# Low parts of 32 expert chunks made beside the merges and read back from DRAM

## The chip, the cores and the metric

The kernel runs on one core of a Trainium2 chip. The core has TensorE (PE, matrix products), VectorE (DVE), ScalarE (ACT) and GpSimd (POOL), each with an instruction queue of its own that is worked off in order; SyncE (SP) only issues transfers. The metric is device microseconds of one execution, less being better; a kernel's time is the median of its runs.

## The reference, cut to what matters

Two transformer blocks in float32. The first mixes a latent attention and a retention branch and then has a layer of 16384 experts, of which each token uses 128 (8 heads x 16). For 512 tokens:

```python
merged = jax.nn.sigmoid(za) * y_a + jax.nn.sigmoid(zr) * y_r
h = h + merged @ w_mix_out
x = rmsnorm(h, g_ffn)
q = (x @ w_peer_q).reshape(T, 8, 128)
# eidx, gates: the 16 best of 128 x 128 pairs of keys for each head
act = gelu(einsum('td,tkd->tk', xt, peer_u[it]))
y = einsum('tk,tkd->td', gt * act, peer_v[it])
```

## The kernel before

Every product is made in float32r, as three products of a high and a low part: an operand's high part is the operand cast to float32r (`hi`), its low part the rest (`lo = x - hi`), and the product is hi x hi + hi x lo + lo x hi. For a weight, `weights` (L226) loads 512 KB into a raw tile, ScalarE casts it to `hi` (L212), and DVE or GpSimd subtracts for `lo` (L213). Raw, high and low tiles have two buffers each. `flip` sends the low parts of ordinary weights to DVE and GpSimd in turn.

The first block runs in this order. After the attention and retention branches (to about 360 us) come the merges: for each of eight chunks of 128 output columns, four weights (`w_za`, `w_mla`, `w_zr`, `w_ret`) are loaded, split and multiplied, and the two gated sums are added and split into `mg` (L873). Then come the mix product with `h1` (the residual, loaded into two slots of the pool `sp_`, which has ten), the norm, and the expert layer's queries.

In the expert layer, the three groups of 128 tokens 0 to 2 are computed densely: all 128 chunks of 128 experts are multiplied (`front`: 24 products of 128 x 384 for one chunk of u, then GELU), weighted with a gate matrix and multiplied with the chunk of v. For the fourth group, 128 rows of u and 128 rows of v are gathered for every token by GpSimd's indirect transfers, and used on DVE (`g_u`, `g_v`).

From about 600 to 1000 us the experts are picked: `topkeys` and `topk` find the best keys (on DVE), and `spread` makes the gate matrices: DVE makes one-hot rows (`oh`, L1111), ScalarE or DVE scales them (L1114, L1116), PE multiplies them (L1119), ScalarE copies the result, and it is stored to DRAM. Beside this run the fronts of chunks 0 to 67, spaced by a count of steps; their low parts of u are all made on GpSimd (`u_of(e, G)`). `fm` reads the low part last, in the third eight of the 24 products.

From about 1040 us the expert loop runs: fronts of the other chunks, products with v, gathers. The order of its instructions on DVE, ScalarE and GpSimd is written out by hand; elsewhere the order of each engine's instructions is settled when the kernel is built. Where one engine needs another's result, it waits on a semaphore, and so does everything behind it in its queue.

Of the kernel before, what the change touches and what calls it, by code (L numbers as in the profile page):

```python
# [9 lines left out]
F32 = mybir.dt.float32  # L10
F32R = mybir.dt.float32r
# [3 lines left out]
OP = mybir.AluOpType  # L15
AX = mybir.AxisListType

P = 128
# [4 lines left out]
D = 1024  # L23
KD = D // P
# [142 lines left out]
def build(tc, A, OUT):  # L167
    nc = tc.nc
    es = ExitStack()
    V, S, G, TE = nc.vector, nc.scalar, nc.gpsimd, nc.tensor  # L170

    def pool(name, bufs=1, stack=es, **kw):
        if kw.get("space") != bass.MemoryType.DRAM:
            kw["reuse_waits"] = "tile"
        return stack.enter_context(tc.tile_pool(name=name, bufs=bufs, **kw))

    cp = pool("cst")
    dp = pool("dram", space=bass.MemoryType.DRAM)
# [10 lines left out]
    def mmps(name="mm"):  # L189
        return bank("mm", name)  # L190
# [14 lines left out]
    ones_sq = cp.tile([P, P], F32, name="ones_sq")  # L205
    G.memset(ones_sq, 1.0)

    flip = [0]

    def split(src, hi, lo, lo_eng=None):  # L210

        S.copy(hi, src)  # L212
        (lo_eng or V).tensor_tensor(lo, src, hi.bitcast(F32), op=OP.subtract)  # L213
# [6 lines left out]
    def load(ap, n, tag="w", queue=nc.sync):  # L220
        wp, words, bufs = wts[tag]
        raw = wp.tile([P, words], F32, name=tag + "r", bufs=bufs)
        queue.dma_start(raw[:, :n], ap)
        return raw

    def weights(ap, n, lo_pool=3, tag="w", raw=None):  # L226

        wp, words, bufs = wts[tag]
        raw = raw or load(ap, n, tag)
        hi = wp.tile([P, words], F32R, name=tag + "h", bufs=2)  # L230
        lo = wp.tile([P, words], F32R, name=tag + "l", bufs=2)
        flip[0] += 1
        if isinstance(lo_pool, int):
            lo_pool = V if flip[0] % lo_pool else G
        split(raw[:, :n], hi[:, :n], lo[:, :n], lo_pool)
        return hi, lo

    def kview(pair, kt, width):
        return tuple([t[:, k * width:(k + 1) * width] for k in range(kt)] for t in pair)

    def wfm(name, c, kt=KD, width=P, c0=0):

        n = kt * width
        return kview(weights(A[name][c][:, c0:c0 + n], n, 2), kt, width)

    def mm3(out, l, r, first, last):
        (lh, ll), (rh, rl) = l, r
# [4 lines left out]
    def fm(out, w, act, c0, t0, n, kt=KD, hooks=(), late=0):  # L252


        for tiles in (range(kt - late), range(kt - late, kt)):
            for i, (a, b) in enumerate(((0, 0), (1, 0), (0, 1)) if late else ((0, 0), (0, 1), (1, 0))):
                for k in tiles:
                    TE.matmul(out, w[a][k][:, c0:c0 + P], act[b][k][:, t0:t0 + n],  # L258
                              start=i == 0 and k == 0, stop=i == 2 and k == kt - 1)
                if i < len(hooks) and not late:  # L260
                    hooks[i]()
            if not late:
                break
# [31 lines left out]
    def ks(t):  # L295

        return [t[:, k] for k in range(t.shape[1])]
# [147 lines left out]
    def two(tp, name="t2", dt=F32):  # L445

        return tp.tile([P, L], dt, name=name, tag="t2")
# [4 lines left out]
    def halves(name, tag, dt=F32):  # L452
        h = [xp.tile([P, 4, L], dt, name=name, tag=tag, bufs=2) for _ in range(2)]
        return h, [h[k // 4][:, k % 4] for k in range(KD)]
# [18 lines left out]
    def half_slot(name, dt=F32):  # L473
        return sp_.tile([P, 4, L], dt, name=name, tag="h")

    def flat(t, n):
        return t.rearrange("p k t -> p (k t)")[:, :n]

    def mtwo(name="m2"):
        return tp.tile([P, L], F32, name=name, tag="m2", bufs=9)  # L480

    src = A["hT"].rearrange("p (k t) -> p k t", k=KD)
    _, h1 = halves("h1", "xa")
# [4 lines left out]
    with tc.manual_schedule(engines={mybir.EngineType.DVE, mybir.EngineType.Activation}):  # L488
        raws = [load(A["w_cq"][0], D, queue=nc.scalar)]
        for k in range(KD):  # L490
            (nc.scalar if k % 2 else nc.sync).dma_start(h1[k], src[:, k])
        raws.append(load(A["w_cq"][1], D))
        wqs = []
        for k in range(KD):
            g = gcol[:, G_MIX + k:G_MIX + k + 1]
            S.activation(u[0][k], h1[k], AF.Copy, scale=g)
            V.scalar_tensor_tensor(u[1][k], h1[k], g, u[0][k].bitcast(F32), op0=OP.mult, op1=OP.subtract)
            if k in (1, KD - 1):
                wqs.append(kview(weights(None, D, V, raw=raws[k // 2 and 1]), KD, P))
# [40 lines left out]
    c = ks(half_slot("ckv", F32R))  # L540
# [6 lines left out]
    x = mtwo()  # L547
# [8 lines left out]
    for t0, t1, m in ((0, NT, P), (NT, NT + 1, M)):  # L556
        h = t1 - t0
        pv = pt[:m, t0 * 32:t1 * 32].rearrange("p (t d) -> p t d", t=h)
        x = mtwo()
# [84 lines left out]
    for h in range(8):  # L644
        b = 64 - h % 2 * 64
# [4 lines left out]
    def fm_pieces(w, pieces):  # L650

        x = two(t2)
        for a, b in pieces:
            ps = mmps()
            fm(ps[:, :b - a], w, hn, 0, a, b - a)
            S.copy(x[:, a:b], ps[:, :b - a])
        return x
# [110 lines left out]
    for h in range(8):  # L768
        x = fm_pieces(wfm("w_rv", h), PIECES)
# [10 lines left out]
        b = h % 2 * 64  # L780
# [65 lines left out]
    for h in range(8):  # L846
        w = wfm("w_rg", h)
# [10 lines left out]
    def gate(name, c, x):  # L858

        w = wfm(name, c)  # L860
        ps = mmps()
        fm(ps, w, hn, 0, 0, T)
        S.activation(x, ps, AF.Tanh, scale=0.5)
        return x

    def gated(name, c, act, kt, x):

        w = wfm(name, c, kt)
        ps = mmps()
        fm(ps, w, act, 0, 0, T, kt)  # L870
        V.scalar_tensor_tensor(x, x, 1.0, ps, op0=OP.add, op1=OP.mult)

    def merged(a, b, mg, d):  # L873
        G.tensor_tensor(a, a, b, op=OP.add)
        S.activation(mg[0][d], a, AF.Copy, scale=0.5)
        V.scalar_tensor_tensor(mg[1][d], a, 0.5, mg[0][d].bitcast(F32), op0=OP.mult, op1=OP.subtract)

    mg = tuple([x for _ in range(2) for x in ks(half_slot(n, F32R)[:, :, :T])] for n in ("mgh", "mgl"))
    for c in range(KD):
        x = gate("w_za", c, two(t2)[:, :T])  # L880
        gated("w_mla", c, oT, 4, x)
        y = gate("w_zr", c, two(t2)[:, :T])
        gated("w_ret", c, yr, KD, y)
        merged(x, y, mg, c)
    sty.close()
    h1 = [x for _ in range(2) for x in ks(half_slot("h1"))]
    for k in range(KD):
# [68 lines left out]
    acts, done_u = {}, []  # L956

    def u_of(e, eng=V):
        return kview(weights(A["u_T"][e], D, eng), KD, P)

    def act_tile(e, side):
        return (tr if side else tp).tile([P, TD], F32, name="act", bufs=15 if side else 19)
# [373 lines left out]
    kt = pool("keytmp", stack=stk)  # L1336
# [22 lines left out]
    for x in range(2):  # L1359
# [8 lines left out]
        for hf in range(2):  # L1368
            w = sp_.tile([P, 8, 256], F32, name="wc1", tag="h")
            nc.sync.dma_start(w.rearrange("p l c -> p (l c)"), A["w_c1"][x][:, hf * 2048:(hf + 1) * 2048])  # L1370
            w1.append(w)
    for br in range(2):
        w = wfm("w_kv", 2 * br)
# [4 lines left out]
        for g in range(2):  # L1378
            a, b = slice(g * 64, g * 64 + 64), slice(64 - g * 64, 128 - g * 64)
# [4 lines left out]
        w = wfm("w_kv", 2 * br + 1)  # L1384
        ps = mmps()
        fm(ps, w, hn, 0, 0, T)
        x = two(t2)[:, :T]
# [8 lines left out]
    w = wfm("w_gn", 0, width=48)  # L1396
# [3 lines left out]
    x = two(t2)[:48, :T]  # L1400
# [158 lines left out]
    for g in range(4):  # L1559
        w = wfm("w_u", g)  # L1560
# [32 lines left out]
    for c in range(KD):  # L1593
        y = gate("w_gm", KD + c, two(t2)[:, :T])
        gated("w_pn", c, ysl, KD, y)
        x = gate("w_gm", c, two(t2)[:, :T])
# [19 lines left out]
    w = kview(weights(A["w_f1"][0], KD * 256, tag="ww"), KD, 256)  # L1616
# [11 lines left out]
    for b in range(4):  # L1628
        f = tuple(ks(slot(n, F32R)) for n in ("fh", "fl"))
        for c in range(4):  # L1630
            if b or c:
                w = kview(weights(A["w_f1"][4 * b + c], KD * 256, tag="ww"), KD, 256)
# [52 lines left out]
```

## Time and profile before

| | |
|---|---|
| median of three runs | 2686.99 us (2679.85 to 2689.2) |
| profiled execution | 2676.28 us |
| its span, first to last instruction | 2674.5 us |
| busy: PE, DVE, ACT, POOL | 2579.5, 1713.8, 1145.0, 914.7 us |
| granted clock of PE, mean | 0.99 of 2.4 GHz |

The profile shows one execution. An engine's busy time is the time in which one of its instructions ran; a share of it says little over the whole kernel, since the stages have different limits. The views below are read by stage. In them, a wait is idle time of an engine just before an instruction, put down to what ended it.

### The profile page before, as it was taken

The numbers are of one execution on the slowest core, as the hardware profiler recorded it, in microseconds if no ns is written. First come the engines' busy times: TensorE is split into PE (matmuls) and PEld (weight loads), VectorE is DVE, ScalarE is ACT, GpSimd is POOL, SyncE is SP. The second block draws the span as 40 slices with busy tenths as digits, with TensorE's granted clock in tenths as the row PEclk, the third lists the DMA queues.
The fourth block names the chain that finished last, engine by engine and source line by source line (L and its number), as shares of the span: only waits on it lengthen the run. The fifth ranks groups of instructions, "written<-read, shape, count | busy, mean of one in ns | idle before, by whom it ended". The sixth has DMA issues, their size and how long they took to land.

```text
span 2674.5 us, 37085 instructions
## 1 busy us (share of the span) xinstructions
PE 2579.5 (96%) x13785; PEld 2217.8 (83%) x13785; DVE 1713.8 (64%) x3405; ACT 1145.0 (43%) x2093; POOL 914.7 (34%) x586
## 2 busy tenths in 40 slices
PE   8899999999899998999999999998999999999998
PEld 7768778889899988888888888886666788887887
DVE  5772442256998993888989888866778421534333
ACT  5552342244577663333333333334667423422322
POOL 2122122325344351565555555521222233211112
PEclk9999999999999999999999999999999999999999
DMA  3322223323356667899999999963110123222221
GB/s 129 97 72 69 66 75 122 121 83 118 105 174 198 181 197 277 330 364 398 405 408 367 345 351 332 334 205 119 53 43 25 61 93 101 104 95 95 95 95 63
DMA packets 177957, 465.80 MB, mean 174 GB/s; under 512 B 15856, under 2 KB 78960, under 8 KB 171120
## 3 DMA queue, kind: packets, MB, share of 16 engines
q1 hardware_dynamic: 136592, 321.26, 35.0%
q0 software_dynamic: 37008, 135.81, 13.7%
q10 hardware_dynamic: 4176, 6.36, 0.8%
q8 instruction: 108, 1.77, 0.3%
q14 instruction: 73, 0.60, 0.1%
HBM read 421.17 MB, written 37.42 MB: 171 GB/s over the span
## 4 chain that ended last, share of the span: by engine, by line
PE 79%; DVE 14%; DMA 3%; ACT 2%; issue 1%; POOL 1%; ACTq 0%; SPq 0%; DVEq 0%; POOLq 0%
PE mm L258 36%; PE py L1200 19%; PE pu L258 13%; DVE oh L1111 3%; PE o L1543 2%; PE tp L1538 1%; DVE xn L368 1%; PE mm L1119 1%; DMA t<-t 1%; DVE oh L1083 1%; DVE oh L1086 1%; PE s L717 1%; DVE ef L1088 1%; DMA wr<-in_u_T_dram 1%; ACT wh L212 0%
## 5 line engine op out<-in xcount | busy, mean ns | idle before, releaser
L213 POOL TENSOR_TENSOR wl<-wr,wh 128x1024 fp32r<-128x1024 f32 (+1 forms) x138 | 339.9, 2464 | 747.4 <-ACT wh L212 339.7
L212 ACT CAST wh<-wr 128x1024 fp32r<-128x1024 f32 (+2 forms) x271 | 273.4, 1010 | 312.0 <-PE mm L258 208.0
L258 PE MATMUL pu<-xf,wh 128*128 128x384 f32 x2048 | 391.4, 342 | 13.3 <-ACT wh L212 8.4
L258 PEld LDWEIGHTS pu<-xf,wh 128*128 128x128 f32 x2048 | 360.8, 190 | 19.8 <-ACT wh L212 9.0
L213 DVE TENSOR_TENSOR wl<-wr,wh 128x1024 fp32r<-128x1024 f32 (+1 forms) x133 | 156.8, 1180 | 200.2 <-ACT wh L212 118.8
L992 POOL DMA_INDIRECT row<-in_u_rows_dram,eg x128 | 188.3, 1471 | 192.6 <-DVE row L997 173.0
L992 POOL DMA_INDIRECT row<-in_v_rows_dram,eg x128 | 194.1, 1516 | 165.3 <-DVE yg L1007 140.1
L1187 ACT CAST ah<-act 128x384 fp32r<-128x384 f32 x128 | 65.9, 514 | 327.1 <-DVE act L1184 304.2
L258 PE MATMUL pu<-xf,wl 128*128 128x384 f32 x1024 | 201.2, 338 | 2.6 <-POOL wl L213 2.6
L1200 PE MATMUL py<-vh,ah 128*128 128x512 f32 x768 | 196.3, 390 | 0.0
L1200 PE MATMUL py<-vl,ah 128*128 128x512 f32 x768 | 195.8, 389 | 0.1
L1200 PE MATMUL py<-vh,al 128*128 128x512 f32 x768 | 195.6, 389 | 0.0
L258 PEld LDWEIGHTS pu<-xf,wl 128*128 128x128 f32 x1024 | 181.4, 188 | 3.5 <-POOL wl L213 3.5
L1200 PEld LDWEIGHTS py<-vl,ah 128*128 128x128 f32 x768 | 144.0, 188 | 30.6 <-DVE vl L1192 0.8
L1192 DVE TENSOR_TENSOR vl<-vr,vh 128x1024 fp32r<-128x1024 f32 x128 | 156.2, 1220 | 20.4 <-ACT vh L1190 20.4
L1200 PEld LDWEIGHTS py<-vh,al 128*128 128x128 f32 x768 | 144.2, 188 | 29.9
L1007 DVE SCALAR_TENSOR_TENSOR yg<-row,ag,yg 128x1024 f32<-128x1024 f32 x127 | 162.9, 1282 | 6.4 <-DMA row<-in_v_rows_dram,eg 4.0
L1200 PEld LDWEIGHTS py<-vh,ah 128*128 128x128 f32 x768 | 143.9, 188 | 25.6
L997 DVE SCALAR_TENSOR_TENSOR row<-row,xg 128x1024 f32<-128x1024 f32 x128 | 152.6, 1220 | 13.0 <-DMA row<-in_u_rows_dram,eg 12.9
L1111 DVE TENSOR_TENSOR oh<-iota,eT 128x1024 f32<-128x1024 f32 x96 | 141.5, 1502 | 10.3 <-PE mm L1119 10.2
L399 DVE TENSOR_TENSOR h<-mm,h 128x512 f32<-128x512 f32 (+1 forms) x54 | 34.1, 631 | 172.6 <-PE mm L258 172.6
L1190 ACT CAST vh<-vr 128x1024 fp32r<-128x1024 f32 x128 | 134.5, 1050 | 17.3 <-PE py L1200 16.5
(477 smaller groups left out, 5093.3 us busy)
## 6 DMA issues: line engine op xcount, KB each, us to landing
wr<-in_u_T_dram SPq DMA_DIRECT2D x128, 512.0 KB
vr<-in_v_rows_dram SPq DMA_DIRECT2D x128, 512.0 KB
wwr<-in_w_f_dram SPq DMA_DIRECT2D x32, 1024.0 KB
gates<-stg SPq DMA_DIRECT2D x24, 1024.0 KB
gin<-gates SPq DMA_DIRECT2D x15, 1536.0 KB
wr<-in_w_gm_dram SPq DMA_DIRECT2D x16, 512.0 KB
ahead<-act SPq DMA_DIRECT2D x41, 192.0 KB
act<-ahead SPq DMA_DIRECT2D x41, 192.0 KB
```

The lines of the kernel that those rows point to most:

```text
L212: S.copy(hi, src)
L213: (lo_eng or V).tensor_tensor(lo, src, hi.bitcast(F32), op=OP.subtract)
L258: TE.matmul(out, w[a][k][:, c0:c0 + P], act[b][k][:, t0:t0 + n], start=i == 0 and k == 0, stop=i == 2 and k == kt - 1)
L992: G.indirect_dma_start(out=r, out_offset=None, in_=src, in_offset=bass.IndirectOffsetOnAxis(ap=eg[:, k:k + 1], axis=0))
L997: V.scalar_tensor_tensor(r, r, 1.0, xg, op0=OP.mult, op1=OP.mult, accum_out=ag[:, k:k + 1])
L1007: V.scalar_tensor_tensor(yg[0], r, ag[:, k:k + 1], yg[0], op0=OP.mult, op1=OP.add)
L1111: V.tensor_tensor(a1, iota[:, None, None, :].to_broadcast([P, 2, 4, P]), eT[:, :2, b0 + q0:b0 + q0 + 4, None].to_broadcast([P, 2, 4, P]), ...
L1187: S.copy(ah, a)
L1190: S.copy(vh, raw)
L1192: V.tensor_tensor(vl, raw, vh.bitcast(F32), op=OP.subtract)
L1200: TE.matmul(py[2 * t + d], x[:, t * P:(t + 1) * P], w[:, d * 512:(d + 1) * 512], start=e == 0 and i == 0, stop=e == P - 1 and i == 2)
L1543: TE.matmul(po[b * 64:b * 64 + 64, :2 * P], vt[:, j, br, g], pT[:, b * 256:b * 256 + 256], start=False, stop=last, skip_group_check=True)
```

## The change

- Before the merges, four staging tiles are set up: two of the tag `xa`, two slots of `sp_`. A DRAM tensor `ulow` holds 32 low parts.
- Beside the merges, for the chunks 0, 2, 4, ..., 62 of u: GpSimd's queue loads the chunk into a staging tile (`low_load`), ScalarE casts it, DVE subtracts in place, and GpSimd's queue stores the low part to `ulow` (`low_part`). Four of these stand in each of the eight passes of the merges.
- The load of chunk j + 3 is issued right behind the store of chunk j. Its buffer is that of chunk j - 1, whose store was issued one chunk earlier.
- During the merges all low parts of weights go to DVE (`lo_mod`), and so does the sum of the two gated parts (L874).
- In the fronts of these 32 chunks, the low part is loaded from `ulow` on GpSimd's queue in place of the subtraction on GpSimd.

```diff
-    flip = [0]
+    flip, lo_mod = [0], [2]
...
-    def weights(ap, n, lo_pool=3, tag="w", raw=None):
+    def weights(ap, n, lo_pool=3, tag="w", raw=None, low=None):
...
+        if low is not None:
+            G.dma_start(lo.bitcast(F32)[:, :n], low)
+            S.copy(hi[:, :n], raw[:, :n])
+            return hi, lo
...
-        return kview(weights(A[name][c][:, c0:c0 + n], n, 2), kt, width)
+        return kview(weights(A[name][c][:, c0:c0 + n], n, lo_mod[0]), kt, width)
...
     def merged(a, b, mg, d):
-        G.tensor_tensor(a, a, b, op=OP.add)
+        V.tensor_tensor(a, a, b, op=OP.add)
...
+    NLOW = 32
+    low_of = {2 * j: j for j in range(NLOW)}
+    ulow = dp.tile([NLOW, P, D], F32, name="ulow")
     mg = tuple([x for _ in range(2) for x in ks(half_slot(n, F32R)[:, :, :T])] for n in ("mgh", "mgl"))
+    stage = [flat(x, 2 * D) for x in halves("stage", "xa")[0] + [half_slot("stage") for _ in range(2)]]
+
+    def low_load(j):
+        G.dma_start(stage[j % 4][:, :D], A["u_T"][2 * j])
+
+    def low_part(j):
+        raw, hi = stage[j % 4][:, :D], stage[j % 4][:, D:].bitcast(F32R)
+        S.copy(hi, raw)
+        V.tensor_tensor(raw.bitcast(F32R), raw, hi.bitcast(F32), op=OP.subtract)
+        G.dma_start(ulow[j], raw)
+        if j + 3 < NLOW:
+            low_load(j + 3)
+
+    for j in range(3):
+        low_load(j)
+    lo_mod[0] = 1 << 30
     for c in range(KD):
         x = gate("w_za", c, two(t2)[:, :T])
+        low_part(4 * c)
         gated("w_mla", c, oT, 4, x)
+        low_part(4 * c + 1)
         y = gate("w_zr", c, two(t2)[:, :T])
+        low_part(4 * c + 2)
         gated("w_ret", c, yr, KD, y)
+        low_part(4 * c + 3)
         merged(x, y, mg, c)
+    lo_mod[0] = 2
...
     def u_of(e, eng=V):
-        return kview(weights(A["u_T"][e], D, eng), KD, P)
+        return kview(weights(A["u_T"][e], D, eng, low=ulow[low_of[e]] if e in low_of else None), KD, P)
```

## Rows read from the trace of the kernel before

**Rows 1.** By stretch: length; busy us (instructions) of five engines; PE clock, DMA share, GB/s.

```profile
360.00:500.00 140.00, 140.00 (x605) 113.33 (x604) 32.11 (x36) 40.17 (x50) 35.17 (x23) 1.00 0.34 110
600.00:660.00 60.00, 60.00 (x349) 59.48 (x348) 34.59 (x199) 24.85 (x32) 33.94 (x14) 1.00 0.36 115
660.00:740.00 80.00, 71.11 (x433) 69.84 (x431) 80.00 (x197) 45.76 (x104) 31.19 (x12) 0.96 0.38 116
660.00:1000.00 340.00, 321.16 (x2055) 315.44 (x2054) 324.68 (x782) 224.52 (x524) 144.49 (x52) 0.99 0.57 169
900.00:1000.00 100.00, 93.27 (x614) 90.75 (x613) 99.90 (x190) 60.54 (x134) 43.46 (x14) 1.00 0.64 186
1060.00:1800.00 740.00, 739.88 (x3569) 651.96 (x3568) 636.14 (x815) 268.65 (x363) 381.39 (x254) 1.00 0.93 349
```

**Rows 2.** Waits, 600 to 1000 us: who waited for whom, us, times, longest.

```profile
ACT oh L1116 <- DVE oh L1111: 76.2, 44, 5.1
...
PE tp L1097 <- DVE ef L1088: 6.8, 1, 6.8
```

**Rows 3.** DVE's groups by shape, 600 to 1000 us: count, busy us, mean ns, idle before.

```profile
L1111 DVE TENSOR_TENSOR oh<-iota,eT 128x1024 f32<-128x1024 f32 x96 | 141.5, 1502 | 10.3 <-PE mm L1119 10.2
L1114 DVE TENSOR_SCALAR oh<-oh,eT 128x128 f32<-128x128 f32 x62 | 29.5, 534 | 0.0
```

**Rows 4.** The same two lines over the kernel: ns least, median, most.

```profile
L1111 DVE TENSOR_TENSOR oh<-iota,eT x96: 1199/1214/3432, 687.4 to 999.1; 128x1024 f32<-128x1024 f32 x96
...
L1114 DVE TENSOR_SCALAR oh<-oh,eT x64: 262/277/2436, 908.2 to 1000.6; 128x128 f32<-128x128 f32 x64
```

**Rows 5.** Timeline near 927 us, DVE and GpSimd: start, us, instruction.

```profile
927.86 2.48 DVE L1056 TENSOR_TENSOR gate<-gate,gs 128x128 f32<-128x128 f32 x1
...
927.02 3.17 POOL L213 TENSOR_TENSOR wl<-wr,wh 128x1024 fp32r<-128x1024 f32 x1 [6.29 <-ACT wh L212]
```

**Rows 6.** GpSimd's groups by shape, 600 to 1000 us.

```profile
L213 POOL TENSOR_TENSOR wl<-wr,wh 128x1024 fp32r<-128x1024 f32 x66 | 178.4, 2705 | 225.3 <-ACT wh L212 146.9 <-PE pu L258 46.1 <-PE mm L1119 29.9
```

**Rows 7.** Instructions on the gathered rows, 1060 to 1800 us: ns least, median, most.

```profile
L992 POOL DMA_INDIRECT row<-in_v_rows_dram,eg x128: 934/1306/1987, 1395.4 to 1752.6; - x128
L1007 DVE SCALAR_TENSOR_TENSOR yg<-row,ag,yg x127: 1276/1285/1287, 1409.7 to 1758.8; 128x1024 f32<-128x1024 f32 x127
```

**Rows 8.** The chain that ended last, in order of time: start, us, what.

```profile
860.71 4.20 PE pu L258 x24
...
866.67 4.20 PE pu L258 x24
...
1027.61 11.73 DMA wr<-in_u_T_dram
```

**Rows 9.** Timeline, two transfers of 512 KB: their issue, and the wait each ended.

```profile
747.81 0.33 SPq L223 DMA_DIRECT2D wr<-in_u_T_dram  x1
...
752.08 1.05 ACT L212 CAST wh<-wr 128x1024 fp32r<-128x1024 f32 x1 [0.78 <-DMA wr<-in_u_T_dram]
...
1750.21 1.30 POOL L992 DMA_INDIRECT row<-in_v_rows_dram,eg  x1 [0.30 <-issue]
...
1756.48 1.28 DVE L1007 SCALAR_TENSOR_TENSOR yg<-row,ag,yg 128x1024 f32<-128x1024 f32 x1 [0.16 <-DMA row<-in_v_rows_dram,eg]
```

**Rows 10.** ScalarE's and DVE's groups by shape, 360 to 500 us.

```profile
L212 ACT CAST wh<-wr 128x1024 fp32r<-128x1024 f32 x22 | 23.1, 1050 | 39.4 <-PE mm L258 39.4
...
L213 DVE TENSOR_TENSOR wl<-wr,wh 128x1024 fp32r<-128x1024 f32 x14 | 17.2, 1226 | 44.4 <-PE mm L258 44.4
```

**Rows 11.** Timeline in the merges: one weight's cast and PE's reads of it and its forerunner.

```profile
414.03 1.05 ACT L212 CAST wh<-wr 128x1024 fp32r<-128x1024 f32 x1 [3.54 <-PE mm L258]
...
415.69 2.02 PE L258 MATMUL mm<-yrh,wh 128*128 128x512 f32 x8
...
421.28 2.02 PE L258 MATMUL mm<-hnh,wh 128*128 128x512 f32 x8
```

**Rows 12.** The residual's first use, 430 to 520 us: ns, first and last start.

```profile
L399 DVE TENSOR_TENSOR h<-mm,h x3: 691/692/694, 505.2 to 516.3; 128x512 f32<-128x512 f32 x3
```

## The prediction

> **What bounds the kernel now.** First the busy time by stretch [rows 1]. TensorE (PE) is the bound nearly everywhere: 140.00 of 140 us beside the merges (360 to 500 us) and 739.88 of 740 in the expert loop from 1060 us. The exception is the stage in which the experts are picked (660 to 1000 us): PE is busy for 321.16 of 340, so 18.84 us are idle, 8.89 of them in the first 80 us and 6.73 in the last 100. In these two stretches VectorE (DVE) is full: 80.00 of 80 and 99.90 of 100. So this stage is where the change can be felt, and 18.8 us is about what it can give there.
>
> Second, what is waited for in this stage [rows 2]: PE waits once for 6.8 us for a reduction of DVE, and ScalarE, which feeds PE, waits 76.2 us for DVE's `oh` of L1111. Third, why DVE is full [rows 3, 4]. An `oh` of L1111 takes 1214 ns as a rule, 1502 on average and 3432 at worst; the small scaling of L1114 takes 277 ns as a rule and 534 on average. The long ones coincide with GpSimd's casts [rows 5]: a DVE subtraction of 128 columns that starts at 927.86 lasts 2.48 us and ends within 0.2 us of the cast that began at 927.02 and lasted 3.17. The two engines shut each other out: an instruction that comes second waits for the other's end.
>
> Priced as average less usual length: L1111 96 x (1502 - 1214) = 27.6 us, L1114 62 x (534 - 277) = 15.9. These two groups alone lose 43.5 us of DVE to the 66 casts that GpSimd makes there [rows 6]: 0.66 us a cast.
>
> **The change part by part.** *The fronts.* For 32 of the first 68 chunks GpSimd's cast (2705 ns on average, [rows 6]) goes and a transfer of 512 KB on its queue comes. Freed on DVE: 32 x 0.66 = 21.1 us. Does a transfer issued by GpSimd shut DVE out as a cast does? In the expert loop GpSimd issues its gathers beside DVE instructions with two operands in SBUF, and 127 of these last 1276 to 1287 ns [rows 7]: no. It is the gathers' issue that stretches, 934 to 1987 ns.
>
> What reaches PE? From below: idle time falls in proportion to the lost DVE time, 21.1 / 43.5 x 18.84 = 9.1 us. From above: all of it, 18.8 us, since 21.1 freed exceeds it. I take 15, nearer the upper end, because the idle stands where DVE has no gap, so a microsecond freed there is handed on until PE is caught up.
>
> Is the low part in time? Its buffer (there are two) is released when PE ends the chunk two before, and it is first read after two thirds of its own chunk. A chunk takes PE 4.20 us, and among the gate matrices chunks start 6.0 us apart (860.71, 866.67) [rows 8]: 2 x 6.0 - 4.2 + 2.8 = 10.6 us. In 600 to 660 us, with 14 casts in 60 us [rows 1], chunks stand nearly back to back: 4.2 + 2.8 = 7.0 us. No row has such a transfer from GpSimd by itself. Nearest: a gather of 512 KB from that queue, issued at 1750.21, ends DVE's wait at 1756.48: 6.3 us [rows 9], in a loop whose DMA share is 0.93 [rows 1]. Below: a load issued by SP takes 4.27 us (747.81 to 752.08) [rows 9]. Above: 11.73 us, in the crowd at 1027.61 [rows 8]. The stage's share is 0.36 to 0.64 and it gains 32 x 0.52 MB over 400 us, 42 GB/s. I take the gather's 6.3 us: inside both windows, by 0.7 us in the tight one. On GpSimd's queue only the odd chunk's cast stands behind, due one chunk later, and the issue (1.3 us for that gather) is shorter than the cast it replaces. I charge 1 us for the few that come late.
>
> The Trainium skill speaks against this queue: its page "SBUF — State Buffer" (section "SBUF: two separate sides") says that a DMA issued by GpSimd needs descriptors which GpSimd writes, that a two-port DVE instruction keeps it from writing them, and that SP's or ScalarE's queue avoids this. The gathers' stretched issue above agrees, 1.05 us at worst; by it about seven low parts in the tight window would be 0.4 us late, and the sum would be 2 us smaller.
>
> *The merges.* Added: 32 loads and 32 stores of 512 KB, 32 casts on ScalarE (1050 ns each, 33.6 us) and 32 subtractions on DVE (1226 ns, 39.2 us) [rows 10]. Moved from GpSimd to DVE: eight low parts of full width (9.8 us), eight of half width (about 0.6 each, 4.9) and eight merge sums of half width (4.9). ScalarE goes from 40 to 74 us of 140, DVE from 32 to 91 [rows 1]: both fit. The weights have room: the one cast at 414.03 is first read by PE at 421.28 [rows 11], 6.2 us after the cast's end. A staging load for which ScalarE has to stand in its queue costs nothing below that; beyond it, every microsecond is PE's. DMA rises from 110 GB/s by 33.6 MB in 140 us, 240, to 350: the expert loop moves 349 with PE full [rows 1].
>
> On GpSimd's queue load j+3 waits for store j-1. At 4.4 us a chunk (140 / 32) and 6.3 us a transfer the wait is 1.9 us, and behind it stand only the next store and load. Then 3 x 4.4 - 1.9 - 6.3 = 5.0 us remain until the load is needed: hidden. If transfers took 11.7 us the loop would go at some 6 us a chunk (two chunks to a store) and the merges would take 190 us instead of 140.
>
> The staging takes the two slots that were free for `h1`, whose first use is at 505.2 [rows 12]. Now `h1` waits until a slot falls free near the merges' end; its 2 MB take 6 us at 349 GB/s. Bounds 0 and 6 us; the first mix product (about 5.6 us, the time between two weights' first reads) covers most of it. I charge 1 us for both ends of the merges.
>
> **Sum.** -15 + 1 + 1 = -13 us. The profiled execution, span 2674.5 and 2676.28 in all, would become 2663; the median shown, 2686.99, lies 10.7 above it and becomes **2674 us**.
>
> **The rivals.**
> *A, low parts too late (slower).* Place: PE's last third of each even chunk. If the transfer takes the 11.7 us of the crowd and its issue 1.3, it is late by 2.4 us among the gate matrices (25 chunks) and by 6.0 back to back (7): 60 + 42 = 102 us at worst, 2776. It eats the gain of 15 from 0.5 us a chunk on, that is from about 11 us of issue and landing. For it: a queue that no row shows at work here, gate stores in flight. Against: 6.3 us at a higher share. With 1 to 2 us late on half the chunks about 2695 to 2705. Chance 0.14.
>
> *B, freed DVE time does not reach PE (no change).* The 34 casts left in the stage may each meet DVE longer, as its waiting work is then denser: at 43.5 / 34 = 1.28 us a cast nothing is freed, and the one of [rows 5] cost 2.2. Also the order on each engine is fixed before the run and is made anew for the changed kernel; it may place gate matrices and chunks less well. The gain is then 0 to 8: 2679 to 2690. Against: 32 blockers fewer, and nothing added to DVE's work here. Chance 0.22.
>
> *C, more than forecast.* PE's granted clock is 0.96 in 660 to 740 us [rows 1], 3.2 us at full speed, which come back if the wait of 6.8 us goes; and the wait of 11.73 us in front of the expert loop [rows 8] may shrink. With all 18.8: up to 30 us, 2657. Chance 0.08.
>
> **Numbers.** My forecast has 0.56: 8 to 20 us gained, its own range 2667 to 2679. What a measurement of this kernel tells from no change is about 0.3%, 8 us. Faster is the forecast and C, 0.64; same is B, 0.22; slower is A, 0.14. The range runs from C's end to what B and the mild part of A give: 2656 to 2694.
>
> **What would show it.** Right: in the picking stage about 34 casts of GpSimd instead of 66, the mean of L1111 near 1350 ns, PE idle for 5 us or less between 660 and 1000 us, and the expert loop that much earlier. Wrong: waits of PE for a DMA into the low part (A); L1111's mean still about 1500 ns (B); PE idle between 360 and 520 us behind ScalarE's casts or `h1`.

## The result, and the profile after

The changed kernel takes 2698.33 us (median of 6 runs, 2697.22 to 2702.97), the kernel before 2683.98 (6 runs, 2679.85 to 2689.2): ratio 1.0058, 95% interval 1.0047 to 1.0068. It is 0.6% slower, where 2674 had been forecast. The profiled execution took 2697.22, with a span of 2695.4. Of all executions of all kernels one, of run 4 below, was of a slower kind (2869.16 us at a mean granted clock of 0.845, its others 0.984 to 0.987), and it is left out.

Where the time went shows when the span is cut at the first or last product of each stage (us, from each profile; all kernels of this study, for later). The merges are counted from the first product that reads `yr`; the first products of their first pass stand already among the last retention chunks:

```
                         start   last retention  merges: yr to      mix and   picking   from there
                                 chunks          its last product   queries             to the end
before                   310.9        45.1            143.0          105.7     397.5      1672.3
after                    315.4        50.4            163.5          105.9     388.1      1672.1
fronts only              319.1        46.6            143.1          106.3     387.1      1672.4
merges only              313.7        50.8            164.3          105.8     397.6      1672.4
staging on GpSimd        314.8        51.1            151.5          117.5     388.0      1671.9
transfers only           314.4        46.2            159.9          105.9     386.5      1673.1
work only                316.9        45.4            146.8          105.2     402.3      1672.2
gate banks               314.8        57.6            159.1          104.9     389.4      1675.9
32 pinned                311.5        44.3            147.3          112.0     388.0      1674.3
16 parts                 319.6        50.9            156.5          105.4     394.9      1671.1
28 pinned                315.2        44.3            147.4          105.5     387.8      1674.8
24 pinned                315.9        44.3            147.4          105.4     392.5      1673.1
24 free, second pass     316.2        44.3            156.9          105.7     391.6      1671.3
24 pinned, second pass   316.3        44.3            143.4          105.7     392.2      1673.0
```

The picking stage gives 9.4 us, the two columns of the merges take 5.3 and 20.5. That is +16.6 with the mix; the medians say +14.3. The first column is not the change's doing: up to there every engine has the same instructions in the same order (but for the first low part that moves from GpSimd to DVE, 128 x 512, at 309.2 us before), and the two executions differ in the granted clock, 0.99 and 0.97 on average up to 340 us.

Windows over the merges and the picking stage of the kernel after, columns as in [rows 1]:

```profile
366.00:386.00 20.00, 17.06 (x64) 12.68 (x64) 9.88 (x12) 9.54 (x13) 7.51 (x11) 0.88 0.82 272
386.00:412.00 26.00, 20.37 (x85) 16.01 (x86) 13.63 (x15) 11.14 (x15) 6.07 (x12) 0.93 0.95 334
412.00:446.00 34.00, 32.13 (x132) 25.54 (x131) 19.75 (x21) 16.35 (x19) 9.06 (x17) 0.95 0.92 325
446.00:480.00 34.00, 30.36 (x123) 24.18 (x124) 20.82 (x23) 15.77 (x20) 7.98 (x15) 0.95 0.95 330
480.00:530.00 50.00, 50.00 (x217) 40.45 (x216) 16.95 (x20) 14.85 (x18) 0.05 (x1) 1.00 0.44 150
...
363.90:370.70 6.80, 5.01 (x14) 3.71 (x14) 3.72 (x7) 3.16 (x5) 2.33 (x3) 0.50 0.96 313
408.30:415.10 6.80, 3.49 (x8) 2.81 (x9) 3.80 (x4) 4.51 (x6) 1.54 (x3) 0.50 0.92 357
459.50:462.90 3.40, 3.40 (x10) 2.65 (x9) 2.61 (x3) 1.71 (x2) 1.09 (x3) 0.50 0.91 277
...
636.00:1024.00 388.00, 376.02 (x2387) 372.40 (x2386) 329.68 (x976) 251.85 (x559) 117.12 (x66) 0.99 0.66 208
```

Before, PE was busy for 140.00 of 140 us there at full clock [rows 1]. Now it is idle for 14.1 of the 114 us to 480, and it has half the clock in three stretches, the rows with 0.50: 17.0 us, in 11.9 of which it works. Half of 11.9, some 6 us, is my estimate of what that costs beside the idle time. From 480 on, with the staging done, it runs without a gap again: the loss belongs to the staging. In the first four rows no engine is full, DVE and ScalarE are at about half their time, and the DMA share is 0.92 to 0.95 in three of them. In the picking stage 18.84 us of idle PE [rows 1] became 12.0.

Waits of PE, then of ScalarE, in 345 to 530 us after (who for whom, us, times, longest):

```profile
PE mm L262 <- ACT t L867: 13.0, 4, 5.5
PE tp L835 <- ACT ry L828: 4.2, 3, 1.8
PE mm L262 <- ACT yrh L212: 1.8, 1, 1.8
...
ACT stage L894 <- DMA stage<-in_u_T_dram: 48.3, 21, 5.7
...
ACT wh L212 <- DMA wr<-in_w_za_dram: 8.3, 2, 4.8
```

PE waits for ScalarE nearly throughout, and ScalarE stands for 48.3 us at staging casts whose load has not landed. How one becomes the other, in the timeline after (the longest gap):

```profile
403.32 1.04 ACT L212 CAST wh<-wr 128x1024 fp32r<-128x1024 f32 x1
...
405.00 1.09 PE L262 MATMUL mm<-oTh,wl 128*128 128x512 f32 x4
...
407.71 1.05 POOL L890 DMA_DIRECT2D stage<-in_u_T_dram  x2 [2.99 <-DMA ulow<-stage]
410.02 1.04 ACT L894 CAST stage<-stage 128x1024 fp32r<-128x1024 f32 x1 [5.66 <-DMA stage<-in_u_T_dram]
410.97 0.59 ACT L867 ACTIVATE t<-mm 128x512 f32<-128x512 f32 x1
...
411.61 2.93 PE L262 MATMUL mm<-hnh,wh 128*128 128x512 f32 x6 [5.52 <-ACT t L867]
```

The `w_za` product had been done since the `w_mla` product behind it began; its tanh is 0.59 us of work. But it stands in ScalarE's queue behind a staging cast, that cast waits 5.66 us for its load, and the `w_zr` product needs the PSUM bank that the tanh empties (there are two). So PE waits 5.52 us, 3.9 of them (406.09 to 410.02) for a transfer with which it has nothing to do. The granted clock falls in this gap: from 408.3 on it is 0.50, that is 1.2 GHz, for 6.8 us, while PE starts again at 411.61. The staging casts run from 336.1 to 473.0 us: the first stand among the last retention chunks, and the last is done 56 us, three passes, before the last merge product, where the program has it in the last pass. The order of the build has moved them ahead. It has also put the first tanh between two of the retention's norms: ScalarE loads its function tables at 361.40, 363.66 and 384.17 us, 1.28 us each, where the kernel before does so once, at 355.9.

The picking stage after, GpSimd's and DVE's groups by shape, and the waits of PE there:

```profile
L1140 DVE TENSOR_TENSOR oh<-iota,eT 128x1024 f32<-128x1024 f32 x96 | 134.5, 1427 | 25.7 <-PE mm L1148 19.5 <-ACT act L1008 3.9 <-ACT oh L1145 2.3
...
L1143 DVE TENSOR_SCALAR oh<-oh,eT 128x128 f32<-128x128 f32 x64 | 18.2, 343 | 0.0
...
L213 POOL TENSOR_TENSOR wl<-wr,wh 128x1024 fp32r<-128x1024 f32 x35 | 103.2, 2947 | 204.5 <-ACT wh L212 117.8 <-PE pu L262 64.8 <-PE mm L1148 13.1
L233 POOL DMA_DIRECT2D wl<-ulow x31 | 17.3, 558 | 68.6 <-PE pu L262 37.2 <-PE mm L1148 27.8 <-DMA wr<-in_u_T_dram 3.6
...
PE pu L262 <- POOL wl L213: 6.6, 3, 3.1
PE tp L1126 <- DVE ef L1117: 4.7, 1, 4.7
...
PE pu L262 <- DMA wl<-ulow: 0.3, 1, 0.3
```

35 casts instead of 66; DVE's two groups are shorter than in [rows 3], and PE waits once, for 0.3 us, for a low part from DRAM.

### The profile page after: what moved, and what is told of

The parts are those of the page before. It is cut to its first block, busy times and chain, and to the rows that moved or that the text cites. A ratio compares the mean times of both kernels' runs of the same rounds, so it can differ in the third digit from the quotient of the medians.

```text
span 2695.4 us, 37271 instructions
## 1 busy us (share of the span) xinstructions
PE 2593.9 (96%) x13785; PEld 2229.5 (83%) x13785; DVE 1746.8 (65%) x3469; ACT 1179.5 (44%) x2127; POOL 839.8 (31%) x618
## 4 chain that ended last, share of the span: by engine, by line
PE 82%; DVE 5%; DMA 5%; issue 3%; ACT 2%; POOL 2%; ACTq 0%; SPq 0%; DVEq 0%; POOLq 0%
PE mm L262 33%; PE py L1229 19%; PE pu L262 17%; PE mm L1148 3%; DMA stage<-in_u_T_dram 2%; PE o L1572 2%; PE tp L1567 1%; DMA t<-t 1%; POOL wl L213 1%; DMA wr<-in_u_T_dram 1%; PE s L721 1%; DVE xn L372 1%; DMA ulow<-stage 1%; PE mm L1052 0%; DMA ahead<-act 0%
## 5 line engine op out<-in xcount | busy, mean ns | idle before, releaser
L213 POOL TENSOR_TENSOR wl<-wr,wh 128x1024 fp32r<-128x1024 f32 (+1 forms) x90 | 232.6, 2585 | 695.5 <-PE mm L262 271.8
L212 ACT CAST wh<-wr 128x1024 fp32r<-128x1024 f32 (+2 forms) x239 | 240.2, 1006 | 265.2 <-PE mm L262 171.4
L213 DVE TENSOR_TENSOR wl<-wr,wh 128x1024 fp32r<-128x1024 f32 (+1 forms) x149 | 172.2, 1156 | 187.0 <-ACT wh L212 135.1
L1221 DVE TENSOR_TENSOR vl<-vr,vh 128x1024 fp32r<-128x1024 f32 x128 | 156.2, 1220 | 20.4 <-ACT vh L1219 20.4
L1140 DVE TENSOR_TENSOR oh<-iota,eT 128x1024 f32<-128x1024 f32 x96 | 134.5, 1427 | 25.7 <-PE mm L1148 19.5
```

The lines of the kernel that those rows point to most:

```text
L1140: V.tensor_tensor(a1, iota[:, None, None, :].to_broadcast([P, 2, 4, P]), eT[:, :2, b0 + q0:b0 + q0 + 4, None].to_broadcast([P, 2, 4, P]), ...
L1221: V.tensor_tensor(vl, raw, vh.bitcast(F32), op=OP.subtract)
```

## The experiments

Theories. **Q**: ScalarE works its queue in order; a staging cast that waits for its load holds up the tanh, weight cast or `ry` behind it, and so PE. **T**: the transfers crowd out the weights' loads, or are too slow for the buffers, wherever the casts stand. **W**: the added casts and subtractions are too much work for ScalarE and VectorE. Ratios are to the kernel before, run again beside each series (medians 2681.67 to 2683.02 us).

**1. Fronts only.** One low part is made, in the middle of the merges, and all even chunks read it; the merges are as before (their sums on GpSimd, `lo_mod` left at 2).

```
-    for j in range(3):
-        low_load(j)
+    low_load(0)
...
-        low_part(4 * c)
+        if c == 4:
+            low_part(0)
...
+        ... low=ulow[0] if e in low_of else None
```

> The fronts' part alone: one low part is made in the middle of the merges, and all 32 even chunks read this one from DRAM on GpSimd's queue (so the low part is that of chunk 0 for all of them). The merges are as before. In the changed kernel the picking stage was 9.4 us shorter than before (397.5 to 388.1 us from the first product of the fronts to the last gate product). If the two halves of the change are independent: 9 to 11 us faster than before, about 2674. If the picking stage gained only because it started later or in another order: within 4 us of before.

Measured 2672.4 us, ratio 0.9962 (0.9948 to 0.9976). Picking takes 387.1 us against 397.5: the gain of the fronts is real, 9 to 10 us.

**2. Merges only.** The low parts are made and stored, and the picking stage makes its own all the same: `u_of` is as before.

> The merges' part alone: the 32 low parts are made and stored as in the changed kernel, but the fronts make theirs on GpSimd as before. Changed against before, the last merge product ended 30.3 us later. If that is the merges' own loss: 26 to 31 us slower than before, about 2712. If part of it was drift from earlier stages: 15 to 25 us.

Measured 2706.37 us, ratio 1.0097 (1.0078 to 1.0116). That is 24.7 us above the kernel before, just under the 26 to 31 expected; by stage the merges take 5.7 and 21.3 us more, picking 397.6 as before. The two halves, -9 and +25, make the whole.

**3. Staging on GpSimd.**

```
-        S.copy(hi, raw)
-        V.tensor_tensor(raw.bitcast(F32R), raw, hi.bitcast(F32), op=OP.subtract)
+        G.tensor_copy(hi, raw)
+        G.tensor_tensor(raw.bitcast(F32R), raw, hi.bitcast(F32), op=OP.subtract)
```

> The changed kernel with the staging's cast and subtraction on GpSimd, so that neither ScalarE nor VectorE waits for a staging load. Theory Q (queue): ScalarE stands in its queue at casts of staged chunks whose loads are late (48.3 us of waits for them in the changed kernel), the tanh that frees PE's bank stands behind, PE waits and its clock falls. Then PE's waits for the tanh (13.0 us) and the falls of the clock go: merges within 5 us of before, 2674 to 2681. Rival T (transfers): the DMA engines are crowded (share 0.89) and weights come late; then the merges stay 15 us or more longer, 2690 or more. Rival W (work on ScalarE and VectorE): as Q here.

Measured 2694.36 us, ratio 1.0046 (1.003 to 1.0063): Q's number missed, and by the number alone it would be T. PE's waits for the tanh are nearly gone, 13.0 to 1.0 us, as Q says, but another cost came. DVE's groups by shape, 340 to 520 us of this run:

```profile
L213 DVE TENSOR_TENSOR wl<-wr,wh 128x1024 fp32r<-128x1024 f32 x24 | 60.5, 2521 | 29.2 <-ACT wh L212 23.9 <-PE mm L262 5.3
L878 DVE TENSOR_TENSOR t<-t,t 128x512 f32<-128x512 f32 x8 | 14.3, 1787 | 0.0
```

A low part of a weight takes DVE 2521 ns here, 1226 in [rows 10]: the two engines shut each other out, as the prediction read from [rows 5]. The weights are then late (ScalarE waits 32 us for `w_za`), and the mix stands behind GpSimd too (11.8 us). So the number says nothing for T either: this run neither supports Q's sum nor refutes its mechanism.

**4. Transfers only.** No cast and no subtraction (both lines of `low_part` go): the loaded chunks are stored as they are.

> The changed kernel without the staging's cast and subtraction: the raw chunk is stored as it came (so the low parts are the whole chunk). Loads and stores are as many as before, and no engine but GpSimd waits for them. Theory Q: the merges lose 4 us at most, 2674 to 2680. Rival T (transfers crowd out the weights): the merges stay 15 us or more longer, 2690 or more. Rival W (work): 2674 to 2680.

Measured 2684.12 us, ratio 1.0013 (1.0001 to 1.0024), 11.7 above the fronts alone: above Q's 2680 and below T's 2690, so both numbers missed. Nearly all of it is one gap. Its timeline, with SP's queue:

```profile
448.72 0.33 SPq L223 DMA_DIRECT2D wr<-in_w_ret_dram  x1
...
469.14 2.39 SPq L915 DMA_DIRECT2D h<-in_hT_dram  x5
471.63 0.38 SPq L223 DMA_DIRECT2D wr<-in_w_za_dram  x1
...
477.66 1.04 ACT L212 CAST wh<-wr 128x1024 fp32r<-128x1024 f32 x1 [20.23 <-DMA wr<-in_w_za_dram]
478.61 0.59 ACT L867 ACTIVATE t<-mm 128x512 f32<-128x512 f32 x1
...
479.25 3.35 PE L262 MATMUL mm<-hnh,wh 128*128 128x512 f32 x7 [12.46 <-ACT t L867]
```

SP stood for 20.0 us at the first load of `h1`, whose slot is a staging buffer in its last store; the load of `w_za` stood behind it, its cast stood on ScalarE, and the tanh behind that. It is the same pattern one queue further, but it is not what the changed kernel lost: there the loads of `h1` come at 476.98 to 485, in the stretch without gaps (the last one ends at 458.25). What the transfers do without it shows in the window ahead of it:

```profile
380.00:446.00 66.00, 66.00 (x286) 53.41 (x286) 23.20 (x26) 19.64 (x25) 16.73 (x33) 1.00 0.95 342
```

PE is busy for 66.00 of 66 us at full clock beside 342 GB/s: transfers at that rate do not by themselves hold PE up, and T does not hold.

**5. Work only.** The casts and subtractions without the transfers (28 loads and 28 stores are left out):

```
-        G.dma_start(ulow[j], raw)
-        if j + 3 < NLOW:
-            low_load(j + 3)
+        if j >= NLOW - 4:
+            G.dma_start(ulow[j], raw)
...
-    for j in range(3):
+    for j in range(4):
...
+        return kview(weights(A["u_T"][e], D, eng), KD, P)
```

> Left out of the staging: 29 of the 32 loads and 28 of the 32 stores. Four chunks are loaded at the start, the 32 casts on ScalarE and 32 subtractions on VectorE are done on them again and again, and only the last four results are stored; the picking stage makes all its low parts itself, as in the kernel before. Theory Q (ScalarE stands in its queue at staging casts whose load has not landed, and the tanh behind them frees PE's bank too late): with nothing to wait for, the merges cost at most 4 us more than before, so 2682 to 2687 us. Theory W (the casts and subtractions themselves are too much for ScalarE and VectorE in the merges): the 25 us of the merges-only run stay, about 2707 us.

Measured 2690.26 us, ratio 1.0023 (1.0013 to 1.0032), above Q's 2687 and far from W's 2707. By stage the merges agree with Q: 0.3 and 3.8 us more than before. The windows of its merges and its picking stage:

```profile
362.00:509.00 147.00, 144.24 (x615) 116.06 (x616) 83.24 (x89) 67.27 (x81) 5.42 (x6) 0.99 0.37 122
...
614.00:1017.00 403.00, 383.17 (x2390) 377.50 (x2390) 364.16 (x982) 249.69 (x557) 174.59 (x66) 0.98 0.54 161
```

DVE 83 and ScalarE 67 us of 147, PE idle for 2.8, though the build packed all 32 casts into 337.6 to 407.1 us: W is out. The rest of its loss stands in a picking stage that makes its low parts as before (402.3 us against 397.5; 19.83 us of idle PE against 18.84, and a clock of 0.98 instead of 0.99); why the clock was lower there is not settled.

**6. Gate banks.** `ps = bank("s", "za")` for `ps = mmps()` in `gate`: the gate products go to the three banks that the retention used, and leave the two of `mm` to the others.

> The changed kernel with the gate products in one of the three PSUM banks that the retention used, so that a late tanh does not hold up the product after the next. Theory Q: PE's 13 us of waits for the tanh and the clock at half behind them go, about 2680 us, between 2676 and 2686. Theory T (the transfers and the weights behind them are what is late): the waits turn up at the next product's weights and the time stays at 2695 to 2700 us.

Measured 2701.19 us, ratio 1.0058 (1.0042 to 1.0075). Q's number missed; the time is 1.2 us above T's range, and the waits stand at weights, as T had said. But the trace shows Q's cause behind them. ScalarE's timeline around two of PE's new gaps:

```profile
406.08 1.04 ACT L894 CAST stage<-stage 128x1024 fp32r<-128x1024 f32 x1 [7.89 <-DMA stage<-in_u_T_dram]
...
408.49 1.04 ACT L212 CAST wh<-wr 128x1024 fp32r<-128x1024 f32 x1
...
433.99 1.04 ACT L894 CAST stage<-stage 128x1024 fp32r<-128x1024 f32 x1 [3.67 <-DMA stage<-in_u_T_dram]
434.94 1.04 ACT L212 CAST wh<-wr 128x1024 fp32r<-128x1024 f32 x1
```

PE's 13.0 us behind the tanh are now 11.6 behind weight casts (3.5 at 409.6, 5.1 at 436.0), and these are late because they stand behind staging casts (56.6 us of waits for loads in all): the loads of the two weights were issued at 398.66 and 422.20, and such a load takes 5.6 us here in the median, while their casts start at 408.49 and 434.94. The bank was only the first place where a standing ScalarE was felt. So the part of Q that named the bank fell; its queue stayed. The run is no clean test, though: 12.5 us of its loss stand among the retention chunks (57.6), where the order of PE's products is another one.

**7. 32 pinned.** The staging as in the change, but each cast is put in ScalarE's queue behind the tanh of its own pass, two behind each:

```
+        ins[0] = S.activation(x, ps, AF.Tanh, scale=0.5).ins
...
-        low_part(4 * c)
+        with tc.issue_after(ins[0]):
+            low_part(4 * c)
```

(and so for the other three). 

> The changed kernel with every staging cast placed in ScalarE's queue behind the tanh of its own pass, two behind each, where it had been placed up to one and a half passes earlier. Theory Q, with the order as the cause: the casts no longer stand among the last retention chunks nor ahead of the tanh that frees the bank; 18 to 25 us of the merges come back and the picking stage keeps its 9, so 2673 to 2681 us. If the work or the transfers as such are the cause, wherever they stand, 2693 to 2700 us.

Measured 2682.22 us, ratio 0.9993 (0.9984 to 1.0003): 16 us less than the change, with the same work and the same bytes. The retention chunks lose nothing (44.3), the merges 4.3 us, ScalarE waits 1.0 us for staging loads instead of 48.3. What it missed Q's 2681 by stands in the mix (+6.3 us). Its timeline there:

```profile
491.45 4.92 SPq L922 DMA_DIRECT2D h<-in_hT_dram  x8
...
496.95 16.51 SPq L223 DMA_DIRECT2D wr<-in_w_mix_dram  x3
...
509.58 1.04 ACT L212 CAST wh<-wr 128x1024 fp32r<-128x1024 f32 x1 [8.49 <-DMA wr<-in_w_mix_dram]
510.53 0.62 ACT L879 ACTIVATE mgh<-t 128x512 fp32r<-128x512 f32 x1
...
511.21 0.50 PE L262 MATMUL mm<-mgh,wh 128*128 128x512 f32 x1 [2.84 <-ACT mgh L879]
```

The last staging cast comes at 500.04, and `h1` is loaded from 491.45 on; its eight loads, the last staging transfers and the mix weights come together. That they delay one another is my reading of it; run 9 tests it.

**8. 16 parts**, those of every fourth chunk, two to a pass, not pinned (`NLOW = 16`, `low_of = {4 * j: j ...}`).

> The changed kernel with 16 low parts, those of every fourth chunk, two to a pass of the merges, where it had 32, four to a pass. If loss and gain both go by the number: 12 us lost in the merges and 4.7 gained in the picking stage, about 2689 us. If the merges lose only because four to a pass come faster than a transfer of 6.9 us plus a store of 6.5 us and the four buffers let them, they lose 0 to 5 us and the time is 2677 to 2683 us.

Measured 2695.83 us, ratio 1.0042 (1.0026 to 1.0057). Half the parts lose 19 us of the 26 and gain 2.6 of the 9.4: both expectations missed. ScalarE's waits for staging loads are halved (25.4 us), but 7.1 us of PE's waits, for `ry` and `yrh`, stand among the retention chunks. The build placed all 16 casts between 340.3 and 418.9 us, one in 5.2 on average. What counts is not the number, it is what stands behind a waiting cast.

**9 and 10. 28 and 24 pinned**: run 7 without parts in the last pass, and in the last two (`if 4 * c + k < NLOW`).

> The pinned run with 28 low parts: the last pass of the merges makes none. If what the pinned run still lost stands at its end (eight loads of h1 and the loads of w_mix together with the last stores, a wait of 8.5 us for w_mix on ScalarE with the last merge behind it, 4.6 us of PE in the mix), the mix starts as before: 5 to 6 us back, 1.2 less gained in picking, 2676 to 2679 us, 0.15 to 0.25% faster than before. If the last stage only shifts what the staging costs anyway, 2681 to 2684 us.

> The pinned run with 24 low parts, none in the last two passes. At 0.3 us gained for a low part and no loss at the end, 1.2 us more than with 28 where the end is free already, so 2677 to 2680 us; if 28 still collide with the loads of h1, which here come one pass earlier, 2674 to 2677 us.

Measured 2674.4 us, ratio 0.9974 (0.9964 to 0.9984), and 2677.94, ratio 0.9986 (0.9977 to 0.9994). With 28 the mix starts as before (105.5 us) and picking keeps 9.7 us: this version beats both kernels, and is 1.6 us under the range expected of it. The next four parts fewer cost 4.7 us in picking, more than the 1.2 reckoned; their time is in the first of the two ranges. The busy windows of 28 pinned, merges and picking:

```profile
359.00:507.00 148.00, 145.35 (x620) 116.43 (x619) 82.66 (x89) 68.70 (x84) 29.92 (x53) 0.99 0.82 288
...
612.00:1000.00 388.00, 376.87 (x2387) 372.31 (x2386) 337.11 (x982) 250.85 (x556) 127.00 (x65) 0.99 0.64 202
```

**11 and 12. 24 parts from the second pass on, free and pinned.** Both begin behind the tanh of the second pass. In the free run that is the only tie; in the other each pair stands behind its own tanh, as in run 7.

```
 # free
+        t = S.activation(x, ps, AF.Tanh, scale=0.5).ins
+        if name == "w_za" and c == 1:
+            ins[0] = t
 # both
+        if 1 <= c <= 6:
+            with tc.issue_after(ins[0]):
+                low_part(4 * c - 4)
```

> 24 low parts as in the run beside this one, but held behind one tanh only, that of the second pass, after the last retention chunk; from there they stand where the build puts them, three and four between two tanh, some of them just ahead of one. If only the start among the retention chunks cost the 25 us, the time is that of the pinned 24, within 3 us. If casts that stand ahead of the tanh cost by themselves: three quarters of the some 18 us that the changed kernel lost after the retention, less 7 gained, so 2687 to 2693 us.

> The same 24 low parts from the second pass on as in the free run, from the same start, but two behind each tanh: beside the free run only the order differs. Theory Q: the three gaps before the products of w_zr or w_za (8.6 us) and the half clock behind them go, 10 to 14 us less than the free run, so 2674 to 2678 us. If the pinned runs were better only because they began earlier and left more time for each transfer, 2684 to 2690 us. Beside the pinned 24 that began with the first pass: the 4 us that pinning still lost in the merges stand at the first pass (1.8 us before a w_zr product, and half clock behind it); if they do, 2 to 4 us less than that run.

Free 2688.22 us, ratio 1.0021 (1.0011 to 1.003); pinned 2675.71, ratio 0.9973 (0.9963 to 0.9984). Both lie in the ranges that go with the order as the cause. They ran on different chips, each beside the kernel before: by the ratios 0.48%, by the medians 12.5 us. Number, start (373.9 and 374.0 us), work and bytes are the same, and on every engine the other instructions stand in the same order up to the end of the merges; only the places of the staging differ. ScalarE stands for 38.1 us at staging loads in the free run and for none in the pinned one, and PE waits 9.4 and 0.8 us for the tanh. The same place in the two timelines, free first:

```profile
394.54 1.09 PE L262 MATMUL mm<-oTh,wl 128*128 128x512 f32 x4
...
398.34 1.04 ACT L897 CAST stage<-stage 128x1024 fp32r<-128x1024 f32 x1 [4.21 <-DMA stage<-in_u_T_dram]
399.29 0.59 ACT L867 ACTIVATE t<-mm 128x512 f32<-128x512 f32 x1
...
399.93 2.50 PE L262 MATMUL mm<-hnh,wh 128*128 128x512 f32 x5 [4.30 <-ACT t L867]
```

```profile
392.81 1.09 PE L262 MATMUL mm<-oTh,wh 128*128 128x512 f32 x4
393.01 0.60 ACT L867 ACTIVATE t<-mm 128x512 f32<-128x512 f32 x1 [0.75 <-PE mm L262]
...
393.50 1.99 ACT L895 CAST stage<-stage 128x1024 fp32r<-128x1024 f32 x2
...
395.59 2.02 PE L262 MATMUL mm<-hnh,wh 128*128 128x512 f32 x8
```

Pinned, the tanh starts 0.20 us after the next product's first matmul, and the two staging casts stand behind it. And their windows (free, then pinned), 400 to 450 us:

```profile
400.00:450.00 50.00, 45.66 (x177) 36.11 (x178) 28.38 (x30) 23.58 (x27) 13.18 (x25) 0.91 0.97 330
```

```profile
400.00:450.00 50.00, 50.00 (x217) 40.55 (x216) 29.16 (x31) 23.29 (x29) 10.69 (x20) 1.00 0.88 305
```

PE is full at 305 GB/s beside the staging. Begun in the second pass, the merges take 143.4 us, as before the change (143.0): the 4 us that the other pinned runs lost stood at the first pass, beside the last retention chunks. In this order 24 parts cost the merges 0.4 us.

With the order goes the pace: the last cast starts at 462.7 us free and at 480.8 pinned, one in 3.9 us against one in 4.6, so the pinned run's transfers have more time. Pace alone is not the cause, since run 8 lost 19 us with one cast in 5.2 us on average and transfers as quick as the pinned run's (load and store 4.5 and 5.3 us in the median, there 4.6 and 6.4); how much of the 12.5 it makes up is not shown.

## Why the prediction was wrong

**The picking stage: right in mechanism, and the size at the lower bound.** I took 15 of 9.1 to 18.8 us; the change gave 9.4, the fronts alone 10.4 in that stage. The DVE time was freed nearly as reckoned: L1140 lost 96 x (1427 - 1214) = 20.4 us (1214 is still its median) and L1143 64 x (343 - 276) = 4.3, together 24.7 where [rows 3] had some 43.5, so 18.8 freed and not 21.1; each remaining cast costs 0.71 us instead of 0.66. PE's idle time fell by 6.8 of the 9.4 us, the rest lies in its busy time. The mis-sized term is what reaches PE: DVE, less hindered, now waits 19.5 us for PE ahead of L1140 (10.2 in [rows 3]), and PE waits 6.6 us for GpSimd's remaining casts, 2.6 before, which were 2705 ns and are 2947. That the idle time would fall "in proportion" was the better of the two bounds.

**Low parts in time: right.** PE waits 0.3 us for them in all, and they take 5.6 us from issue to landing in the median, where 6.3 was forecast; rival A did not happen. The rule from the Trainium skill, page "SBUF — State Buffer" (section "SBUF: two separate sides"), by which I had made seven of them late, did not show here: these issues take 558 ns on average, without the stretching of the gathers in [rows 7]. The page speaks of two-port DVE instructions; that DVE's instructions here, or those beside the gathers, are of that kind is something I assumed and no run shows.

**The merges: wrong, and this turned the sign.** Three sentences failed, and the third stands on the second.

"Hidden", with 5.0 us to spare for a load. This took the store's wait as the only thing between two uses of a buffer and an even pace. A round of a buffer is a cast of 1.04, a subtraction of 1.23, a store of 6.3 and a load of 6.9 us (medians after; 6.3 was forecast for both), 15.5 us, against 4 x 4.4 = 17.6: some 2 us to spare, and only for casts evenly spread. In the build's order they are not: 21 of 32 stood waiting, 48.3 us in all.

"A staging load for which ScalarE has to stand in its queue costs nothing below that", that is, below the 6.2 us of [rows 11]. These are the slack of one weight cast. I priced one customer of a queue that has others: the tanh, `ry`, `yrh`, `mgh`. Nearest behind the waiting cast stood the tanh, whose cover is the `w_mla` product of 2.8 us; for `ry` and `yrh`, among the retention chunks, PE waited 6.0 us in all. In the gap shown PE had ended that product at 406.09, the load that the cast waited for let ScalarE go on at 410.02, and after the cast and the tanh PE began at 411.61. That the engine takes its queue strictly in order is also what the Trainium skill says (page "TensorE: Matmul & The Clock Gate", the table of specifications at its head, row on the queue depth); the trace agrees in the gap shown, where the tanh starts (410.97) as the cast that stood ahead of it ends (410.02 + 1.04), and run 6 shows another customer, the weight cast, paying in the tanh's place.

"I charge 1 us for both ends of the merges." I looked at `h1` at the rear end and not at the front, where the first casts ran ahead into the retention chunks: 5.3 us there. The loads of `h1` did not hurt the changed kernel; in run 7, where the staging ends later, the mix lost 6 us beside them, which came back when the last pass was left free (run 9).

Sum as measured: -9.4 in picking, +5.3 at the retention, +20.5 in the merges (some 13.6 of it idle PE, 14.1 against 0.5, and some 6 half clock), +0.2 in the mix: +16.6 in the profiles and +14.3 in the medians, where -15 + 1 + 1 stood. (The forecast also set the median 10.7 us above the profiled execution, from three runs; with six it is 2683.98, 7.7 above.) Rival B had named the cause in passing, the order made anew at build, but only for the picking stage; and the list of what would show the forecast wrong ended with "PE idle between 360 and 520 us behind ScalarE's casts", which is what came. No rival had it, and no chance was given to it.

**What is shown and what is not.** That the order in which the build puts the staging on ScalarE costs 12.5 us with 24 parts is shown by runs 11 and 12, which differ in the places of the staging alone (and so in its pace, see there); for the 32 of the change, run 7 beside it gives some 16 and, with the end set free (run 9, 28 parts), some 23. That the work (W) is not the cause is shown by run 5's merges and by run 12. That the transfers (T) are not is shown by run 4's 66 us at 342 GB/s and by run 12. How the 5.3 us among the retention chunks divide between casts that wait and the two table loads more is open, as are run 5's longer picking stage, and why picking took 392.5 us with 24 parts and 387.8 with 28.

## What to carry to other kernels

Work that waits for a transfer, put on an in-order engine that also serves the bound engine, is not priced by its duration or by one neighbour's slack, but by the least slack of everything that can stand behind it; where the build chooses the order, tie such work behind the instruction that must not wait. Then look at both ends of the stretch: at the front for instructions that run ahead into the stage before, at the rear for buffers that the next stage's loads are waiting for. Here that turned a loss of 0.6% into a gain of 0.3% with the same instructions, less four of 32 low parts.

## What the runs showed of the hardware

The gaps cost more than their length: in the gap of 5.5 us PE's granted clock falls to 0.50 at 408.3 us and stays there for 6.8 us, and from 366 to 480 us it is 0.88 to 0.95 on average, where the kernel before had 1.00; by the estimate above that is some 6 us beside 14.1 of idle time. A transfer of 512 KB from GpSimd's queue takes 6.9 us as a load and 6.3 as a store at a DMA share of about 0.9 (medians of the kernel after), and PE is not slowed by them: 66.00 of 66 us at clock 1.00 beside 342 GB/s in run 4.
